# Opening layer 1's output projection with causal heads' tiles, and transposing the memory's probabilities into the scores' banks

## The chip, the core and the metric

One core of a Trainium2 chip runs the kernel as one launch. The metric is device microseconds (us) of that core. The engines named below are TensorE (PE: matmuls and transposes; PEld is its weight load), VectorE (DVE), ScalarE (ACT), GpSimd (POOL) and SyncE (SP, which here only issues transfers). PE writes its results into PSUM, eight banks of 128 partitions x 512 floats; ACT and DVE read them from there into SBUF.

## What is computed

The reference is a trunk of two layers over 256 positions of width 1024. Each layer has a mixer and, beside it, a 4-head cross-attention into 256 memory tokens; their outputs stand side by side, an output projection multiplies them, and a LayerNorm and a SwiGLU channel mixer follow. Layer 1's mixer is causal attention with 12 heads of 64 (256 positions are a single block, so it is plain causal attention):

```
q, k, v, q_mem = jnp.split(x @ b_w_in, [768, 1536, 2304], axis=-1)
mix     = causal_attention(q, k, v)                  # 12 heads x 64 -> 768 columns
mem_out = memory_cross_attention(q_mem, mem, w_kv)   # 4 heads x 64 -> 256 columns
sub = jnp.concatenate([mix, mem_out], axis=-1) @ w_mix_out
x = layer_norm(ALPHA * x + sub)
x = layer_norm(ALPHA * x + swiglu(x, w_ffn_in, w_ffn_out))
```

## The kernel before

Everything is float32, done on PE in reduced-precision passes: an operand is split into a high part (ACT, line 221) and a low part (DVE, line 222, which needs the high part), and a product takes three matmuls, high x high, high x low, low x high (`PASSES`). So each weight half of 128 x 1024 costs ACT and DVE one instruction each, and so does each activation tile. PE's order is the order of the code; the other engines' orders are set by a scheduler when the kernel is built, and each engine takes its instructions strictly in its order.

PSUM is two groups of four banks. `mm_tile` gives a bank of the group `mm` (projections, transposes, attention outputs), `acc_tile` one of the group `acc` (scores, the K projections, the output projection's sums). A new tile takes a bank whose tile before has been read by its last reader, and waits for that reader.

Layer 1's attention runs over six pairs of heads, i = 0 to 5 ("block i" below), in this order on PE: `qk_half(i, 0)`, the pair's Q (tile `qk`, 24 matmuls); `att_t(i-2)`, six transposes of the pair's probabilities (`pt`, line 849), which ACT copies to SBUF (`pT`, 851); `scores(i-1)`, two tiles `s` of five matmuls each, of which the second multiplies by `klq`, the low part of K that DVE makes (447); `qk_half(i, 1)`, the pair's K; `att_pv(i-2)`, the output `pv` of a pair, split into the pair's tile `mix` by ACT and DVE. The softmax of a score tile is maxima `mb` on DVE (370), exponentials `pb` on ACT (372) and a normalisation on DVE (377).

The memory's four heads are woven in: scores `sm` in blocks 1 and 3, eight transposes `ptm` (line 397, two tiles) in blocks 2 and 4, each copied by ACT to `pTm` (400), and in block 5 `mem_pv`, 16 matmuls `pvm`, whose two tiles become mix 6 and mix 7.

Then comes the output projection `OutProj(1, mix, "c")`, tile `opc`. For each half of the positions (`tt`) it adds up eight products, k = 0 to 7: k = 0 to 5 read the causal pairs' mix tiles, 6 and 7 the memory's. `op.step(tt, ks)` issues six matmuls for each k of the list; `op.close` issues the last two k and the LayerNorm. Pairs 4 and 5 are not done when it begins, so their transposes, scores and outputs are woven between its steps. The channel mixer (`pg`, `Xg`, `Yg`, `Zg`, `fog`) follows, then the last LayerNorm.

Of the kernel before, what the change touches and what calls it, by code (L numbers as in the profile page):

```python
# [208 lines left out]
def build(nc, tc, ins, out):  # L209
    ET = mybir.EngineType  # L210
    with (
# [15 lines left out]
        def mm_tile(name):  # L227
            return ps.tile([P, 512], F32, tag="mm", name=name)

        def work_tile(name):  # L230
            return actp.tile([P, 512], F32, tag="work", name=name, bufs=9)
# [122 lines left out]
        def load_gb(l, which):  # L354
            t = actp.tile([P, 2, D], F32, tag="gb", name=f"gb{l}{which}")
            nc.sync.dma_start(t[:, 0, :], bcast_row(ins[f"ln_{which}_g"][l, :], D))
            nc.sync.dma_start(t[:, 1, :], bcast_row(ins[f"ln_{which}_b"][l, :], D))
            return t
# [21 lines left out]
        def mem_scores(qa, k, nm, psum_tile, hs=range(4)):  # L380
            ka, kl = k
            pr = []
            for h in hs:
                c, par = h // 2, h % 2
                s = psum_tile[h - hs[0]](f"s{nm}{h}")
                for q in range(2):
                    score_mms(s[:, q * 256:(q + 1) * 256], qa[c][:, par, q * P:(q + 1) * P], ka[c][:, par, :], kl[:, c, par, :])
                pr.append(Softmax(s, [(0, 256), (256, 512)], f"{nm}{h}"))
            return pr

        def mem_transposes(pr, nm, hs=range(4)):
            pts = []
            for h in hs:
                t = mm_tile(f"ptm{nm}{h}")
                for q in range(2):
                    for k in range(2):
                        nc.tensor.transpose(t[:, k * 256 + q * P:k * 256 + (q + 1) * P],
                                            pr[h].p[:, q * 256 + k * P:q * 256 + (k + 1) * P], ident)
                sb = work_tile(f"pTm{nm}{h}")
                nc.scalar.copy(sb, t)  # L400
                pts.append(sb)
            return pts

        def mem_pv(pts, vm, mix, nm):
            for pair in range(2):
                o = mm_tile(f"pvm{nm}{pair}")
                for k in range(2):
                    for j in range(2):
                        h = 2 * pair + j
                        mm(o[HD * j:HD * j + HD, :T], vm[:, k, h * HD:(h + 1) * HD], pts[h][:, k * 256:(k + 1) * 256],  # L410
                           k == 0, k == 1)
                split(mix[6 + pair][:, 0, :], mix[6 + pair][:, 1, :], o[:, :T])
# [318 lines left out]
        for j in range(4):  # L731
            t = actp.tile([P, 2, 512], F32R, tag="hm", name=f"memT{j}", bufs=4)
# [28 lines left out]
        pr = mem_scores(qm, km, "m0", (acc_tile, acc_tile, mm_tile, mm_tile))  # L761
# [4 lines left out]
        op = OutProj(0, mix, "a")  # L766
# [5 lines left out]
        gb = load_gb(0, "mix")  # L772
        op.step(0, [2, 3, 4, 5])
        pts = mem_transposes(pr, "0")
        op.step(1, [0], first=True)
        mem_pv(pts, vm, mix, "0")
# [40 lines left out]
        def qk_half(hp, j):  # L817
            t = (acc_tile if j else mm_tile)(f"qk{hp}{j}")[:, :T].rearrange("p (j t) -> p j t", j=1)
            ws_proj(t, f"qk{hp}", xs, (j,))
            t = t[:, 0, :]  # L820
            if j == 0:
                st = actp.tile([P, 2, 512], F32R, tag="hm", name=f"qks{hp}", bufs=4).rearrange("p a (b t) -> p a b t", b=2)
                qks[hp] = st, klq[:, hp % 2]
                stack_q(lambda par: st[:, 0, par, :], t)
            else:
                stream.done(f"qk{hp}")
                st, kl = qks[hp]
                stack_k(lambda par: st[:, 1, par, :], kl, t)

        def scores(hp):  # L830
            st, kl = qks[hp]
            ss = []
            for par in range(2):
                s = acc_tile(f"s{hp}{par}")
                q, k = st[:, 0, par, :], st[:, 1, par, :]
                mm(s[:, 0:128], q[:, 0:128], k[:, 0:128], True, False)
                mm(s[:, 0:128], q[:, 0:128], kl[:, par, 0:128], False, False)
                mm(s[:, 128:384], q[:, 128:256], k, False, False)
                mm(s[:, 128:384], q[:, 128:256], kl[:, par], False, False)
                mm(s.rearrange("p (b t) -> p b t", t=256)[:, :, 0:128], identb, maskb.to_broadcast([P, 2, P]), False, True)  # L840
                ss.append(s)
            return [Softmax(s, [(0, 128), (128, 384)], f"b{hp}{j}") for j, s in enumerate(ss)]

        def att_t(hp):
            pts = []
            for j in range(2):
                t = mm_tile(f"pt{hp}{j}")
                for c in range(3):
                    nc.tensor.transpose(t[:, c * P:(c + 1) * P], prs[hp][j].p[:, c * P:(c + 1) * P], ident)
                sb = work_tile(f"pT{hp}{j}")  # L850
                nc.scalar.copy(sb[:, :384], t[:, :384])
                pts.append(sb)
            return pts

        def att_pv(hp):
            o = mm_tile(f"pv{hp}")
            for j in range(2):
                h = 2 * hp + j
                rows = slice(j * HD, (j + 1) * HD)
                mm(o[rows, 0:256], vt[:, 0, h * HD:(h + 1) * HD], pTs[hp][j][:, 0:256], True, False)  # L860
                mm(o[rows, 128:256], vt[:, 1, h * HD:(h + 1) * HD], pTs[hp][j][:, 256:384], False, True)
            split(mix[hp][:, 0, :], mix[hp][:, 1, :], o[:, :256])

        pts, pr_mem = [], []
        for i in range(6):
            qk_half(i, 0)
            if i >= 2:
                pTs[i - 2] = att_t(i - 2)
            if i >= 1:
                prs[i - 1] = scores(i - 1)  # L870
                for p in prs[i - 1]:
                    p.normalise()
            qk_half(i, 1)
            if i >= 2:
                att_pv(i - 2)
            if i in (1, 3):
                pr_mem += mem_scores(qm, km1, "m1", (acc_tile, acc_tile), (i - 1, i))
                for p in pr_mem[i - 1:]:
                    p.normalise()
            if i in (2, 4):  # L880
                pts += mem_transposes(pr_mem, "1", (i - 2, i - 1))
            if i == 2:
                gb = load_gb(1, "mix")
            if i == 4:
                mix += [actp.tile([P, 2, T], F32R, tag=f"mix{k}", name=f"mix1_{k}") for k in range(6, KT)]
            if i == 5:
                mem_pv(pts, vm1, mix, "1")
        op = OutProj(1, mix, "c")
        op.step(0, [6, 7], first=True)
        pTs[4] = att_t(4)  # L890
        prs[5] = scores(5)
        for p in prs[5]:
            p.normalise()
        op.step(0, [0])
        att_pv(4)
        op.step(0, [1])
        pTs[5] = att_t(5)
        op.step(0, [2])
        att_pv(5)
        op.step(1, [6], first=True)  # L900
        op.step(0, [3])
        op.close(0, [4, 5], xres, gb)
        op.step(1, [7, 0, 1, 2, 3])
        x3T = actp.tile([P, KT, 2, T], F32R, tag="xT", name="x3T")
# [81 lines left out]
```

## Time and profile before

| | us |
|---|---|
| median of 3 runs | 573.89 (573.73 to 576.27) |
| the profiled execution, its own time | 573.57 |
| span of its trace | 571.8 |
| PE busy | 558.6 (98% of the span) |
| DVE busy | 486.5 (85%) |
| ACT busy | 349.5 (61%) |

The span is the time from the first to the last instruction of the trace; the execution's own time holds 1.77 us more around it. Positions in the trace are counted from the span's start. PE's busy share counts a matmul as busy to its modelled end; matmuls overlap, so the next one starts a little before the one ahead of it ends.

### The profile page before, as it was taken

Reading aid. Unit: us, or ns where it says so; the run is one execution under the profiler, and the core shown is the slowest. Engines: PE = TensorE matmul, PEld = TensorE weight load, DVE = VectorE, ACT = ScalarE, POOL = GpSimd, SP = SyncE. Lnnn points to the kernel's source line nnn. Section 1 sums busy time; section 2 is a strip of 40 time slices with the busy share of each in tenths; the row PEclk is TensorE's granted clock in tenths of the full one; section 3 lists DMA queues with packets and bytes.
Section 4 is the critical chain, followed back from the end, with each engine's and each line's share of the span. In section 5 each row is a group of like instructions: output and inputs, shape, how many; then the busy total and the mean of one; then the engine's idle time right before and its main releaser. Section 6 shows DMA issues by size and latency. Waiting matters only on the chain.

```text
span 571.8 us, 8069 instructions
## 1 busy us (share of the span) xinstructions
PE 558.6 (98%) x3088; PEld 483.1 (84%) x3088; DVE 486.5 (85%) x649; ACT 349.5 (61%) x536; POOL 14.8 (3%) x24
## 2 busy tenths in 40 slices
PE   8999999999999999999999998899999999999994
PEld 7999879888888888888999997688888888888884
DVE  5797989999898998974987887489999999989726
ACT  6766957758647655852476988455656676558400
POOL 2020000000000000000100000000000000000001
PEclk9999999999999999999999999999999999999998
DMA  8997686416914932864476323247009629528002
GB/s 299 388 339 292 230 331 238 175 56 237 384 41 151 364 148 76 295 217 148 159 285 246 120 88 134 74 143 286 15 17 394 250 74 359 230 83 285 0 1 73
DMA packets 20182, 110.49 MB, mean 193 GB/s; under 512 B 2224, under 2 KB 5424, under 8 KB 8752
## 3 DMA queue, kind: packets, MB, share of 16 engines
q1 hardware_dynamic: 19856, 109.72, 52.0%
q8 instruction: 24, 0.39, 0.3%
q10 hardware_dynamic: 288, 0.26, 0.1%
q14 instruction: 14, 0.11, 0.1%
HBM read 108.92 MB, written 1.05 MB: 192 GB/s over the span
## 4 chain that ended last, share of the span: by engine, by line
PE 89%; ACT 4%; DVE 4%; issue 1%; DMA 1%; SPq 0%; POOLq 0%; ACTq 0%
PE fof L245 10%; PE pf L245 10%; PE pg L245 10%; PE fog L245 9%; PE Xf L245 6%; PE Xg L245 6%; PE opc L245 4%; PE opa L245 4%; PE pu L245 3%; PE bv L245 3%; PE Zg L245 3%; PE Zf L245 3%; PE va L245 3%; PE pvm L245 2%; PE hkm L245 2%; PE hqm L245 2%
## 5 line engine op out<-in xcount | busy, mean ns | idle before, releaser
L221 ACT CAST spl_s_M<-raw_s 128x1024 fp32r<-128x1024 f32 x84 | 86.7, 1054 | 52.9 <-DVE raw_s L179 23.3
L222 DVE TENSOR_TENSOR spl_s_M<-raw_s,spl_s_M 128x1024 fp32r<-128x1024 f32 x84 | 100.4, 1222 | 7.5 <-ACT spl_s_M L221 7.3
L245 PE MATMUL fof<-spl_w,htf 128*128 128x512 f32 x264 | 62.8, 390 | 0.0
L222 DVE TENSOR_TENSOR spl_w<-raw_w,spl_w 128x1024 fp32r<-128x1024 f32 x44 | 53.7, 1224 | 6.8 <-ACT spl_w L221 5.6
L245 PEld LDWEIGHTS fof<-spl_w,htf 128*128 128x128 f32 x264 | 49.4, 188 | 10.2
L179 DVE TENSOR_TENSOR raw_s<-raw_s,raw_s 128x1024 f32<-128x1024 f32 x48 | 57.0, 1220 | 0.0
L221 ACT CAST spl_w<-raw_w 128x1024 fp32r<-128x1024 f32 x44 | 46.1, 1053 | 15.9 <-PE fof L245 5.0
L245 PE MATMUL fog<-spl_w,htg 128*128 128x512 f32 x228 | 54.2, 390 | 0.0
L245 PEld LDWEIGHTS fog<-spl_w,htg 128*128 128x128 f32 x228 | 42.7, 188 | 8.8
L245 PE MATMUL qk<-x2T,spl_qk 128*128 128x256 f32 x288 | 36.7, 285 | 0.0
L245 PEld LDWEIGHTS qk<-x2T,spl_qk 128*128 128x128 f32 x288 | 35.2, 192 | 0.0
L245 PE MATMUL pf<-spl_r_A,x1T 128*128 128x512 f32 x120 | 29.2, 394 | 0.0
L245 PE MATMUL pg<-spl_r_A,x3T 128*128 128x512 f32 x120 | 29.1, 392 | 0.0
L245 PE MATMUL pg<-spl_r_B,x3T 128*128 128x512 f32 x120 | 28.9, 391 | 0.0
L221 ACT CAST spl_r_B<-raw_r_B 128x1024 fp32r<-128x1024 f32 x20 | 21.1, 1053 | 12.4 <-PE opc L245 6.2
L245 PE MATMUL pf<-spl_r_B,x1T 128*128 128x512 f32 x120 | 28.3, 389 | 0.0
L245 PEld LDWEIGHTS pf<-spl_r_B,x1T 128*128 128x128 f32 x120 | 22.5, 188 | 4.7
L222 DVE TENSOR_TENSOR spl_r_B<-raw_r_B,spl_r_B 128x1024 fp32r<-128x1024 f32 x20 | 24.4, 1219 | 2.4 <-ACT spl_r_B L221 2.3
L245 PEld LDWEIGHTS pg<-spl_r_B,x3T 128*128 128x128 f32 x120 | 22.4, 188 | 4.6
L245 PEld LDWEIGHTS pg<-spl_r_A,x3T 128*128 128x128 f32 x120 | 22.3, 188 | 4.5
L245 PEld LDWEIGHTS pf<-spl_r_A,x1T 128*128 128x128 f32 x120 | 22.2, 188 | 4.6 <-PE pvm L245 0.2
L245 PE MATMUL opc<-spl_o,mix 128*128 128x512 f32 x96 | 23.7, 399 | 1.7 <-ACT mix L221 1.7
(235 smaller groups left out, 1097.0 us busy)
## 6 DMA issues: line engine op xcount, KB each, us to landing
raw_s<-in_w SPq DMA_DIRECT2D x24, 1024.0 KB, 5.4
raw_w<-in_w SPq DMA_DIRECT2D x22, 1024.0 KB, 5.3
raw_r_A<-in_w SPq DMA_DIRECT2D x10, 1024.0 KB, 5.6
raw_r_B<-in_w SPq DMA_DIRECT2D x10, 1024.0 KB, 4.8
raw_o<-in_w SPq DMA_DIRECT2D x8, 1024.0 KB, 6.2
raw_qk<-in_w SPq DMA_DIRECT2D x6, 1024.0 KB, 4.8
raw_u<-in_w SPq DMA_DIRECT2D x3, 1024.0 KB, 9.7
raw_bv<-in_w SPq DMA_DIRECT2D x4, 768.0 KB, 4.3
```

Source lines behind the costliest of these rows:

```text
L179: self.nc.vector.tensor_add(raw, raw, self.raw[parts[1]][:, sl])
L221: nc.scalar.copy(hi, src)
L222: nc.vector.tensor_sub(lo, src, hi.bitcast(F32))
L245: nc.tensor.matmul(o, lhsT, rhs, start=start, stop=stop, skip_group_check=on)
```

## The change

It does two things. In blocks 2 and 4 the memory's transposes `ptm` take their PSUM tiles from the group `acc` in place of `mm` (layer 0's stay in `mm`). And the steps of the output projection's first half stand in another order: k = 0 and 1 open it where 6 and 7 did, then 2, 3, 6 and 7 stand at the four later places where 0, 1, 2 and 3 stood. The second half's order (6, then 7, 0, 1, 2, 3) and both closings stay.

```diff
-        def mem_transposes(pr, nm, hs=range(4)):
+        def mem_transposes(pr, nm, hs=range(4), psum_tile=mm_tile):
             pts = []
             for h in hs:
-                t = mm_tile(f"ptm{nm}{h}")
+                t = psum_tile(f"ptm{nm}{h}")
...
             if i in (2, 4):
-                pts += mem_transposes(pr_mem, "1", (i - 2, i - 1))
+                pts += mem_transposes(pr_mem, "1", (i - 2, i - 1), acc_tile)
...
         op = OutProj(1, mix, "c")
-        op.step(0, [6, 7], first=True)
+        op.step(0, [0, 1], first=True)
         pTs[4] = att_t(4)
         prs[5] = scores(5)
         for p in prs[5]:
             p.normalise()
-        op.step(0, [0])
+        op.step(0, [2])
         att_pv(4)
-        op.step(0, [1])
+        op.step(0, [3])
         pTs[5] = att_t(5)
-        op.step(0, [2])
+        op.step(0, [6])
         att_pv(5)
         op.step(1, [6], first=True)
-        op.step(0, [3])
+        op.step(0, [7])
         op.close(0, [4, 5], xres, gb)
```

The number of instructions is the same on every engine, and the orders of ACT, DVE, POOL and SP are the same. On PE the steps move, and the semaphores for which its instructions wait change.

First place, on PE: the end of block 4 and the start of block 5, from the second memory tile's first transpose to block 5's K projection, with the semaphores that a row waits for in brackets (most rows without a wait are left out; `ident` is the unit matrix, `pm` and `pb` are the memory's and the pairs' probabilities). Before:

```order
L397 MATMUL ptm_3395<-ident,pm_3256 128x128 [waits DVE_49,PE_49]
L245 MATMUL qk_3404<-x2T,spl_qk_0_3405 128x256 [waits DVE_49]
L849 MATMUL pt_3442<-ident,pb_3330 128x128 [waits DVE_49]
L849 MATMUL pt_3448<-ident,pb_3337 128x128 [waits Activation_49]
L245 MATMUL s_3454<-qks_3301 128x128
L245 MATMUL s_3460<-qks_3301 128x128
L245 MATMUL s_3460<-klq,qks_3301 128x128 [waits DVE_49]
L245 MATMUL qk_3486<-x2T,spl_qk_0_3405 128x256 x12
```

With the change:

```order
L397 MATMUL ptm_3395<-ident,pm_3256 128x128 [waits DVE_49,PE_49,Activation_49]
L245 MATMUL qk_3404<-x2T,spl_qk_0_3405 128x256 x12
L849 MATMUL pt_3442<-ident,pb_3330 128x128 [waits DVE_49] x2
L849 MATMUL pt_3448<-ident,pb_3337 128x128 [waits DVE_49] x2
L245 MATMUL s_3454<-qks_3301 128x128 [waits PE_49,Activation_49]
L245 MATMUL s_3454<-klq,qks_3301 128x128 [waits DVE_49]
L245 MATMUL s_3460<-qks_3301 128x128 [waits Activation_49]
L245 MATMUL s_3460<-klq,qks_3301 128x128 [waits DVE_49]
L245 MATMUL qk_3486<-x2T,spl_qk_0_3405 128x256 [waits Activation_49]
```

Before, the first `pt` waits until DVE has split `pv` of pair 2 and the second until ACT has copied the first `ptm` tile; with the change both wait for their own probabilities alone. In their place the second `ptm` tile waits until ACT has read the score tile of pair 3 (its exponentials), the second score tile until ACT has copied the first `ptm` tile, and the K projection until it has copied the second. Block 2 changes in the same way at its `ptm`.

Second place, on PE: the end of `mem_pv` and the start of the output projection, again without most of the rows that wait for nothing. Before:

```order
L245 MATMUL pvm_3531<-pTm_3400,svm_1143 64x256
L245 MATMUL opc_3538<-spl_o_3_0_3566,mix_6_3402 128x512 [waits Activation_49]
L245 MATMUL opc_3538<-spl_o_3_0_3566,mix_6_3402 128x512 [waits DVE_49]
L245 MATMUL opc_3538<-spl_o_3_1_3575,mix_7_3403 128x512 [waits Activation_49]
L245 MATMUL opc_3538<-spl_o_3_1_3575,mix_7_3403 128x512 [waits DVE_49]
L849 MATMUL pt_3586<-ident,pb_3466 128x128 x3
L849 MATMUL pt_3592<-ident,pb_3473 128x128 [waits PE_49]
```

With the change:

```order
L245 MATMUL pvm_3531<-pTm_3400,svm_1143 64x256
L245 MATMUL opc_3538<-spl_o_0_0_3542,mix_0_2779 128x512
L245 MATMUL opc_3539<-spl_o_0_0_3542,mix_0_2779 128x512 [waits PE_49,Activation_49]
L245 MATMUL opc_3538<-spl_o_0_1_3551,mix_1_2780 128x512
L849 MATMUL pt_3562<-ident,pb_3466 128x128 [waits DVE_49] x2
L849 MATMUL pt_3568<-ident,pb_3473 128x128 [waits DVE_49]
L245 MATMUL s_3574<-qks_3437 128x128 [waits Activation_49]
```

The four waits for the high and low parts of mix 6 and 7 are gone from the opening. The second matmul's wait is for pair 4's exponentials, the second `pt` tile's for DVE's low part of mix 3.

## Rows read from the trace of the kernel before

**Rows 1.** The page: busy time by engine, and the last chain's shares.

```profile
PE 558.6 (98%) x3088; PEld 483.1 (84%) x3088; DVE 486.5 (85%) x649; ACT 349.5 (61%) x536; POOL 14.8 (3%) x24
...
PE 89%; ACT 4%; DVE 4%; issue 1%; DMA 1%; SPq 0%; POOLq 0%; ACTq 0%
```

**Rows 2.** Chain that ended last: start, us, what; two of the pieces before 359.

```profile
315.96 0.97 PE sm L245 x8
...
358.61 0.38 ACT mix L221
```

**Rows 3.** Windows: length, busy us of each engine, granted clock, DMA share, GB/s.

```profile
345.00:359.00 14.00, 10.80 (x91) 9.16 (x89) 11.33 (x27) 12.61 (x35) 0.00 (x0) 1.00 0.22 81
```

**Rows 4.** Timeline of PE: start, duration, line, operation, idle time before and releaser.

```profile
344.17 1.09 PE L397 MATMUL ptm<-ident,pm 128*128 128x128 f32 x8
...
348.72 0.55 PE L849 MATMUL pt<-ident,pb 128*128 128x128 f32 x3 [0.59 <-DVE mix L222]
350.16 0.55 PE L849 MATMUL pt<-ident,pb 128*128 128x128 f32 x3 [0.90 <-ACT pTm L400]
...
351.19 0.28 PE L245 MATMUL s<-klq,qks 128*128 128x128 f32 x1
...
351.64 3.11 PE L245 MATMUL qk<-x2T,spl_qk 128*128 128x256 f32 x24
...
355.38 1.90 PE L245 MATMUL pvm<-pTm,svm 128*64 128x256 f32 x16
359.03 3.22 PE L245 MATMUL opc<-spl_o,mix 128*128 128x512 f32 x12 [1.74 <-ACT mix L221]
362.08 0.82 PE L849 MATMUL pt<-ident,pb 128*128 128x128 f32 x6
...
366.19 1.69 PE L245 MATMUL opc<-spl_o,mix 128*128 128x512 f32 x6
367.71 0.82 PE L849 MATMUL pt<-ident,pb 128*128 128x128 f32 x6
```

**Rows 5.** Timeline of ACT, block 4 to the projection's start.

```profile
344.46 0.46 ACT L372 ACTIVATE pb<-s,mb 128x256 f32<-128x256 f32 x1
...
349.52 1.07 ACT L400 COPY pTm<-ptm 128x512 f32<-128x512 f32 x2
...
358.61 0.65 ACT L221 CAST mix<-pvm 128x256 fp32r<-128x256 f32 x2
```

**Rows 6.** Timeline of DVE in the same stretch.

```profile
350.01 0.43 DVE L447 TENSOR_TENSOR klq<-qk,qks 64x256 fp32r<-64x256 f32 x1
...
359.30 0.42 DVE L222 TENSOR_TENSOR mix<-pv,mix 128x256 fp32r<-128x256 f32 x1
359.64 0.75 DVE L222 TENSOR_TENSOR mix<-pvm,mix 128x256 fp32r<-128x256 f32 x2
```

**Rows 7.** The chain in the channel mixer: one piece of 24 matmuls.

```profile
410.01 5.44 PE fog L245 x24
```

**Rows 8.** Timelines in block 2: ACT's exponential and copies, PE's transposes.

```profile
325.44 0.46 ACT L372 ACTIVATE pb<-s,mb 128x256 f32<-128x256 f32 x1
...
330.82 0.84 ACT L851 COPY pT<-pt 128x384 f32<-128x384 f32 x2
...
329.04 0.82 PE L849 MATMUL pt<-ident,pb 128*128 128x128 f32 x6
```

**Rows 9.** Timelines after the projection's start: who feeds PE, and how early.

```profile
372.35 1.05 ACT L221 CAST spl_r_B<-raw_r_B 128x1024 fp32r<-128x1024 f32 x1 [1.21 <-PE opc L245]
...
409.41 0.69 DVE L222 TENSOR_TENSOR htg<-tpg,htg 128x512 fp32r<-128x512 f32 x1
...
410.75 0.62 PE L245 MATMUL fog<-spl_w,htg 128*128 128x512 f32 x2
...
428.81 1.22 DVE L222 TENSOR_TENSOR spl_s_M<-raw_s,spl_s_M 128x1024 fp32r<-128x1024 f32 x1
...
433.44 0.39 PE L245 MATMUL Xg<-spl_s_M,SgM 128*128 128x512 f32 x1
```

## The prediction, as it stood before the run

> **What bounds the kernel now.** I read the page first: PE is busy for 98% of the span and holds 89% of the chain that ended last, ACT and DVE 4% each [rows 1]. So a microsecond counts only where PE waits, and the next question is where the chain leaves PE. It does so in layer 1's attention: after the memory's scores, a piece that ends at 316.93, no PE piece stands on the chain until ACT's split of mix 6 ends at 358.99 and the projection starts [rows 2]. In between PE runs ahead of ACT and DVE, and pays at the end. In the window 345 to 359 PE is busy 10.80 of 14 us, ACT 12.61, and TensorE's granted clock stays at 1.00, its level of 2.4 GHz, so the idle time has no second price in clock [rows 3]. PE's timeline names the three waits: 0.59 us before `pt` for DVE's split of mix 2, 0.90 before the second `pt` for ACT's copy `pTm`, 1.74 before the first `opc` for ACT's mix 6 [rows 4]. They add up to 3.23 us; after the projection's start I found no further one, and the chain is PE again.
>
> **The opening of the projection.** It waited for mix 6 and needs mix 0 and 1 now, whose pairs were split in blocks 2 and 3; the weight halves it reads were made before too, and no DMA moves, since SP's order is the same. `pvm` starts at 355.38 and its modelled end is 357.28; `opc`'s row shows how much earlier than that a successor starts: it ends at 362.25, while `pt` stands at 362.08, 0.17 before. So `opc` could have started at 357.11 and started at 359.03: 1.92 us go [rows 4]. The twelve matmuls then took 3.05 us start to start, with a second small wait inside for mix 6's low part (DVE's row of both low parts begins at 359.64) [rows 6]. Six unhindered ones take 1.52 (366.19 to 367.71), and six more at the channel mixer's pace, 24 in 5.44 us, take 1.36 [rows 4, 7]. That is 2.88 in place of 3.05: another 0.17. Bounds: 0 and 0.33, twelve at 2.72. The new second matmul's wait, for pair 4's exponentials, costs nothing, since ACT has gone on from them to the splits of mix 6 and 7 by 358.61 [rows 5] and had them done before it took up the weight casts between.
>
> **The waits in blocks 4 and 5.** The two waits before `pt` go; others stand in their place. ACT and DVE keep their orders, and nothing in this stretch lets them start earlier: their chain is their own [rows 2]. So I hold their times and move PE alone. ACT copies the two `ptm` tiles from 349.52 to 350.59 [rows 5], the first one ending just before the `pt` at 350.16 that waited for it [rows 4]. With the change PE does both `pt` and the first score tile before that, but the second score tile now wants that very bank: it too starts at about 350.16. Its second matmul wants `klq`, done at 350.44 [rows 6]; with the 0.05 us from release to start it goes at 350.49 in place of 351.19 [rows 4]. The K projection behind it comes out at 350.94, later than the second copy's end, so that its own new wait is covered by 0.35 us. Worth: **0.70**, not the 1.49 of the two waits. Bounds: 0 (the K projection or the score tile held until its old time) and 1.49.
>
> **What the new banks cost.** In block 4 the second `ptm` tile waits for ACT's exponentials of pair 3, which end at 344.92; the eight transposes begin at 344.17, so the fifth came at about 344.66, and some 0.3 us are lost [rows 4, 5]. They fall in front of the wait until 350.16 and are absorbed by it. In block 2 the same exponential ends at 325.90, and again about 0.3 us are lost on PE. PE is not on the chain there: the next thing ACT takes from it, the `pt` tiles that end at 329.86, lies ready for 0.96 us before ACT copies them at 330.82 [rows 8]. So I cost both at nothing; with that cover gone they would be 0.6.
>
> **What is late next.** With `opc` 0.70 + 1.92 us earlier, at 356.41, and 2.88 long, the transposes of pair 4 start at 359.29. The second of their tiles waits for DVE's low part of mix 3, done at 359.72 [rows 6]; PE gets there at about 359.6, so with a restart this costs 0.20, and what stands behind it, pair 5's scores and the rest of the steps, is late by as much. Bound: 0 to 0.4. After that the old distances hold: mix 6 and 7, whose low parts end at 360.39 [rows 6], are read some 4 us later, and the pieces between two steps have the same lengths as before.
>
> **Does the rest follow?** ACT waits for PE at 372.35, for a weight buffer to come free [rows 9], so the feeding of the channel mixer starts earlier with PE. If it did not: the tightest weight half I found is done at 430.03 and used at 433.44, 3.4 us of room [rows 9], more than is gained. The tightest loop through DVE is shorter: `htg`'s low part ends at 410.10 and is used at 410.75, 0.65 us [rows 9]; it begins with PE, so it should move as a whole.
>
> **The sum.** 0.70 + 1.92 + 0.17 - 0.20 = 2.59 us. From the execution's own 573.57 (span 571.8 and 1.77 around it) that leaves 570.98; from the median, 0.32 higher, 571.30. I predict **571.2**. With the terms at their bounds it is 0 + 1.74 + 0 - 0.4 = 1.34 (572.2) to 1.49 + 1.92 + 0.33 = 3.74 (569.8).
>
> **Rivals.** *All waits go* (569.8): the copies of `ptm` no longer hold anything, because the tiles have banks of their own. The Trainium skill, page "Perfetto Trace Analysis", section "Optimizing Tensor Performance", says so: independent matmul groups should rotate through PSUM banks so that the evacuation of one overlaps the next group's matmuls; by that the block-4 term would be 1.49 where the rows give 0.70. Against it: the bank that the second score tile and the K projection take is the one that ACT empties at 350.10 and 350.59, and ACT is busy 12.61 of those 14 us [rows 3, 5]. The rotation only moves the wait to another tile.
>
> *Given back later* (572.9): if DVE's work in the channel mixer did not move with PE, the loop with 0.65 us of room would take back 1.94. DVE's 85% [rows 1] speaks for it, ACT's wait for PE at 372.35 against.
>
> *No effect* (573.6): some wait that I don't see takes the opening's place. The new one on pair 4's exponentials would be it, and ACT's order speaks against.
>
> *Slower*: the second `ptm` copy becomes what PE waits for. Before, that copy held nothing until `pvm`; now the K projection of pair 5 stands behind it, and behind that `pv`, `pvm` and the whole projection. Each microsecond that ACT comes to it later than 350.94 goes onto the end. It decides from 0.35 + 2.59 = 2.94 us of delay on; 6 us would give 576.6. For it speaks that ACT is the busiest engine there but PE; against it that no instruction of ACT or DVE before the copy waits for anything that the change delays by more than 0.3 us, with 0.96 us of room in block 2 [rows 8].
>
> **Numbers.** My forecast 0.66 (own range 570.5 to 571.9), all waits go 0.10, given back 0.14, no effect 0.06, slower 0.04. The range takes the forecast, the first rival and most of the second: 569.8 to 572.9. A measurement of this kernel tells about 0.5%, 2.87 us, from no change; the forecast stands just inside it at 2.59. I give it one chance in five to be over that, 0.13, and with the first rival faster comes to 0.23; slower 0.03, three quarters of that rival; the rest, 0.74, is the same.
>
> **What would show it.** Right: no idle time before the first `opc`; the wait of 0.9 before the second `pt` gone and a new one of some 0.4 to 0.8 before the second score tile, released by ACT's `pTm`, with `klq` behind it; the first `opc` near 356.4, the first step between 366 and 372 some 2.6 us earlier; ACT's copies still at 349.5 and mix 6 at 358.6. The forecast falls if those ACT times move (then its chain did depend on PE), if PE shows idle time after 372, or if the K projection starts at 351.6 as before.

## The result, and the profile after

The changed kernel takes **571.12 us** (median of 8, 570.58 to 571.95) where the kernel before takes 573.83 (median of 8), ratio 0.9947 with an interval of 0.9934 to 0.9960. Two more series of it gave 571.31 and 571.00 (ratios 0.9948 and 0.9940). 571.2 was forecast. All three intervals lie below 1, so the changed kernel is faster, by about half a per cent; the prediction took 0.5% for the least that can be told from no change, and the gain stands right at that.

Executions of one and the same kernel differ by some 3 us, in those with a profile mostly because the first weights land at another time in each (the last section shows the largest case). This lies ahead of everything that the change touches. In the profiles it can be taken off: the first `sm` matmul of layer 1's memory scores stands ahead of the change's first instruction, and the distance from it to the span's end holds no start. In 11 of the 14 profiles this matmul stands 306.96 to 307.00 us behind the first one on the low part of the second weight piece, wherever that one is. Kernel before and kernel after, PE's timeline at that matmul (start, duration, what):

```profile
315.79 0.28 PE L245 MATMUL sm<-kkm,qqm 128*128 128x256 f32 x1
```

```profile
315.41 0.28 PE L245 MATMUL sm<-kkm,qqm 128*128 128x256 f32 x1
```

With the spans of 571.8 and 568.8 the distances are 256.01 and 253.39 us: **2.62 us** by the change, and 0.38 of the 3.0 between the two spans by the start. Two more profiles of the changed kernel, with the first `sm` at 316.17 and 315.86, give 253.43 and 253.44. The distance repeats within 0.05 us, which is also how far a span, given to 0.1 us, can be off. So below it is the measure for what the clock times can't tell apart.

The page of after: busy time, and the shares of the chain that ended last [answers to rows 1].

```profile
PE 559.4 (98%) x3088; PEld 484.2 (85%) x3088; DVE 486.4 (86%) x649; ACT 349.7 (61%) x536; POOL 15.3 (3%) x24
...
PE 93%; DVE 3%; ACT 2%; DMA 1%; issue 1%; SPq 0%; POOLq 0%; ACTq 0%
```

Window of 14 us at the same place, 0.38 earlier [rows 3]: length, busy us of PE, PEld, DVE, ACT, POOL, then granted clock, DMA share, GB/s.

```profile
344.62:358.62 14.00, 13.66 (x105) 11.77 (x104) 11.36 (x27) 12.61 (x34) 0.00 (x0) 1.00 0.22 85
```

PE is busy 13.66 of the 14 us, not 10.80; ACT's busy time is the same 12.61. PE's timeline of after [rows 4]:

```profile
344.16 1.13 PE L397 MATMUL ptm<-ident,pm 128*128 128x128 f32 x8
345.05 3.11 PE L245 MATMUL qk<-x2T,spl_qk 128*128 128x256 f32 x24
348.00 0.82 PE L849 MATMUL pt<-ident,pb 128*128 128x128 f32 x6
348.57 0.30 PE L245 MATMUL s<-qks 128*128 128x128 f32 x1
...
349.73 0.33 PE L245 MATMUL s<-qks 128*128 128x128 f32 x1 [0.33 <-ACT pTm L400]
350.07 0.33 PE L245 MATMUL s<-klq,qks 128*128 128x128 f32 x1
...
350.56 3.11 PE L245 MATMUL qk<-x2T,spl_qk 128*128 128x256 f32 x24
353.60 0.88 PE L245 MATMUL pv<-pT,vt 128*64 128x256 f32 x8
354.30 1.90 PE L245 MATMUL pvm<-pTm,svm 128*64 128x256 f32 x16
356.14 3.02 PE L245 MATMUL opc<-spl_o,mix 128*128 128x512 f32 x12
358.99 0.91 PE L849 MATMUL pt<-ident,pb 128*128 128x128 f32 x6
359.66 0.30 PE L245 MATMUL s<-qks 128*128 128x128 f32 x1
...
360.25 0.31 PE L245 MATMUL s<-qks 128*128 128x128 f32 x1
360.39 0.28 PE L245 MATMUL s<-klq,qks 128*128 128x128 f32 x1
...
360.83 1.63 PE L245 MATMUL opc<-spl_o,mix 128*128 128x512 f32 x6
```

Of the three waits none is left; one of 0.33 stands before the second score tile, released by ACT's copy `pTm` (the prediction named 0.4 to 0.8 as its sign). The first `opc` waits for nothing. ACT's timeline [rows 5]:

```profile
349.09 1.07 ACT L400 COPY pTm<-ptm 128x512 f32<-128x512 f32 x2
...
358.19 0.65 ACT L221 CAST mix<-pvm 128x256 fp32r<-128x256 f32 x2
```

Both are 0.42 or 0.43 earlier than before, which is the start's 0.38 and 0.05: ACT kept its own pace while PE moved by 2.6.

### The profile page after: what moved, and what is told of

It is laid out like the page before. It is cut to its first block, busy times and chain, and to the rows that moved or that the text cites. A ratio compares the mean times of both kernels' runs of the same rounds, so it can differ in the third digit from the quotient of the medians.

```text
span 568.8 us, 8070 instructions
## 1 busy us (share of the span) xinstructions
PE 559.4 (98%) x3088; PEld 484.2 (85%) x3088; DVE 486.4 (86%) x649; ACT 349.7 (61%) x536; POOL 15.3 (3%) x24
## 4 chain that ended last, share of the span: by engine, by line
PE 93%; DVE 3%; ACT 2%; DMA 1%; issue 1%; SPq 0%; POOLq 0%; ACTq 0%
PE fof L245 11%; PE pf L245 10%; PE pg L245 10%; PE fog L245 9%; PE Xg L245 6%; PE Xf L245 6%; PE opc L245 4%; PE opa L245 4%; PE qk L245 4%; PE pu L245 3%; PE bv L245 3%; PE Zf L245 3%; PE Zg L245 3%; PE pvm L245 3%; PE va L245 3%; PE hkm L245 2%
## 5 line engine op out<-in xcount | busy, mean ns | idle before, releaser
L221 ACT CAST spl_r_A<-raw_r_A 128x1024 fp32r<-128x1024 f32 x20 | 20.7, 1050 | 6.2 <-PE opa L245 4.3
```

Of the source, the lines that this page charges most:

```text
L221: nc.scalar.copy(hi, src)
```

## The experiments

"First sm" is its start in the run's profile, "distance" the span less that start, "gain" 256.01 less the distance. The first four ran beside 17 runs of the kernel before (median 573.77), the next four beside 17 (574.12), the last four beside 16 (574.64). These three medians differ although the kernel is one, so the ratios of different groups are not compared.

| kernel | median us | ratio, interval | first sm | distance | gain |
|---|---|---|---|---|---|
| banks only | 575.04 | 1.0011, 0.9999 to 1.0023 | 315.77 | 255.93 | 0.08 |
| order only | 571.75 | 0.9960, 0.9945 to 0.9975 | 316.11 | 253.99 | 2.02 |
| the change again | 571.31 | 0.9948, 0.9935 to 0.9962 | 316.17 | 253.43 | 2.58 |
| K first | 571.00 | 0.9945, 0.9932 to 0.9959 | 316.68 | 253.22 | 2.79 |
| four more in block 2 | 571.80 | 0.9963, 0.9950 to 0.9976 | 316.48 | 254.02 | 1.99 |
| copies twice | 572.42 | 0.9979, 0.9964 to 0.9995 | 318.81 | 254.39 | 1.62 |
| opening of three | 572.29 | 0.9979, 0.9965 to 0.9994 | 316.16 | 254.14 | 1.87 |
| one tile in acc | 571.14 | 0.9951, 0.9936 to 0.9966 | 315.56 | 253.44 | 2.57 |
| K between | 571.74 | 0.9957, 0.9942 to 0.9972 | 315.91 | 254.09 | 1.92 |
| four more in block 4 | 570.99 | 0.9939, 0.9925 to 0.9953 | 315.87 | 253.43 | 2.58 |
| eight more in block 4 | 571.16 | 0.9945, 0.9931 to 0.9960 | 315.99 | 253.41 | 2.60 |
| the change, third time | 571.00 | 0.9940, 0.9928 to 0.9953 | 315.86 | 253.44 | 2.57 |

### Half of the change: the banks alone

```diff
-        op.step(0, [0, 1], first=True)
+        op.step(0, [6, 7], first=True)
...
-        op.step(0, [2])
+        op.step(0, [0])
...
-        op.step(0, [3])
+        op.step(0, [1])
...
-        op.step(0, [6])
+        op.step(0, [2])
...
-        op.step(0, [7])
+        op.step(0, [3])
```

> The banks of the change with the old order of the steps (the projection opens with mix 6 and 7). Theory (the terms of the prediction): the two waits before pt go and the second score tile's wait takes their place, so TensorE is about 0.7 us further at pvm; but the first opc still waits for ACT's mix 6, which ACT makes at 358.6 whatever TensorE does, so the wait before opc grows from 1.74 to about 2.4 us and the time stays at 573.8 (gain 0, at most 0.2). Rival (the parts add up, each wait removed is worth its length): 0.7 us less, 573.1.

PE's timeline of it, the last product of the attention and the projection's start:

```profile
354.64 1.90 PE L245 MATMUL pvm<-pTm,svm 128*64 128x256 f32 x16
358.94 3.19 PE L245 MATMUL opc<-spl_o,mix 128*128 128x512 f32 x12 [2.40 <-ACT mix L221]
```

`pvm` stands 0.72 earlier than before (38.87 behind the first `sm`, before 39.59), and the wait for mix 6 has grown by 0.66 to 2.40. What was won in block 5 is waited away at the projection: a gain of 0.08, hardly more than the reading's error. The theory holds. The clock times say it too, once they are looked at one by one: 5 of the 12 lie at 573.3 to 573.6 and 7 at 575.0 to 576.1, where of the 17 of the kernel before 14 lie at 573.4 to 574.1 and 3 at 575.0 to 575.4; so its median fell among the upper ones. The profiled execution, 573.44, is of the lower.

### The other half: the order alone

```diff
-                pts += mem_transposes(pr_mem, "1", (i - 2, i - 1), acc_tile)
+                pts += mem_transposes(pr_mem, "1", (i - 2, i - 1))
```

> The new order of the steps with the old banks. Theory: the waits of 0.59 and 0.90 us before pt stay, the 1.74 before opc goes, opc starts at about 357.1 by the positions of the kernel before, its twelve matmuls take 2.88, and the pt behind them come at 360.0, after DVE's low part of mix 3, so that no wait stands there: 1.92 + 0.17 = 2.09 us less, 571.7. Rival 1 (the parts add, so what the whole change gave over the banks' 0.7 is the order's): 573.8 - 1.9 = 571.9, with a wait before pt. Rival 2 (the banks give nothing): as the whole change, 571.1.

PE's timeline of it:

```profile
349.04 0.55 PE L849 MATMUL pt<-ident,pb 128*128 128x128 f32 x3 [0.59 <-DVE mix L222]
350.47 0.55 PE L849 MATMUL pt<-ident,pb 128*128 128x128 f32 x3 [0.89 <-ACT pTm L400]
...
355.69 1.90 PE L245 MATMUL pvm<-pTm,svm 128*64 128x256 f32 x16
357.53 3.02 PE L245 MATMUL opc<-spl_o,mix 128*128 128x512 f32 x12
360.38 0.81 PE L849 MATMUL pt<-ident,pb 128*128 128x128 f32 x6
362.13 1.63 PE L245 MATMUL opc<-spl_o,mix 128*128 128x512 f32 x6
```

The two waits of block 5 stand as before, the opening has none, and neither have the `pt` behind it (1.75 to the next `opc`, as before). 2.02 us of gain, 2.09 expected. So the parts don't add: 0.08 and 2.02 alone, 2.6 together. The banks are worth 0.6 only when the projection no longer waits for the memory.

### The changed kernel again

> The changed kernel itself once more, timed beside the others. Theory: of the 3.0 us between the two profiled executions 0.4 came from the landing of the second raw_v piece at the start (it differs from run to run), 2.6 from the change: 571.2, ratio 0.9955; in its profile the last opc piece before the channel mixer lies 2.6 us earlier than before, once the difference at the start is taken off. Rival: the change gives 3.0 by itself: 570.8, ratio 0.9947, and 3.0 in the profile after the start is taken off.

> The changed kernel once more, beside the version with K between the score tiles: 571.2, and counted from the first sm the last piece of opc 2.6 us earlier than in the kernel before, whatever the first sm's own place is. Rival (the place of the first sm and the gain hang together): another distance than in the two profiles of it that there are.

2.58 and 2.57 at two other starts, 571.31 and 571.00 in clock time: the change gives 2.6, and the rest of the 3.0 between the first two profiles came from the start.

### The copies' hold taken away, or doubled

```diff
-                t = psum_tile(f"ptm{nm}{h}")
+                t = (mm_tile if (nm, h) == ("1", 2) else psum_tile)(f"ptm{nm}{h}")
```

> The change, but block 4's first ptm tile takes its bank from mm again and only the second from acc: then the second score tile no longer waits for ACT's first copy. Theory (the prediction's: klq stands right behind): the second pt tile waits for DVE's low part of mix 2 some 0.2 to 0.4 us, the score tile's second matmul still starts with klq, and from there all is as in the change: gain 0 to 0.1. Rival (all waits go, once no copy holds a bank): the 0.33 and what stands behind it go, 0.3 to 0.5 us less than the change, 570.8.

PE's timeline of it, block 5:

```profile
348.11 0.89 PE L849 MATMUL pt<-ident,pb 128*128 128x128 f32 x6
...
350.23 0.33 PE L245 MATMUL s<-klq,qks 128*128 128x128 f32 x1 [0.58 <-DVE klq L447]
...
350.72 3.11 PE L245 MATMUL qk<-x2T,spl_qk 128*128 128x256 f32 x24
```

The six `pt` hardly wait (0.89 for 0.82, where 0.2 to 0.4 were expected). The second score tile's first matmul is free, its second waits for `klq` at 34.67 behind the first `sm`, where it stood at 34.66 with the change, and the K projection starts at 35.16 after 35.15. Nothing is won: behind the copy stands `klq`, which DVE makes from what ACT has split.

```diff
-                nc.scalar.copy(sb, t)
+                for _ in range(2 if nm == "1" and h in (2, 3) else 1):
+                    nc.scalar.copy(sb, t)
```

> The change, with ACT's two copies of block 4's ptm tiles made twice, one behind the other: the order on ACT is first, second, first, second, so each bank comes free some 1.0 us later. Theory (this stretch still goes at ACT's pace after the change): the second score tile starts 1.0 us later, its wait grows from 0.33 to about 1.3, and all behind it is 0.95 to 1.05 us later: 572.2. Rival (the copies hold nothing until 2.94 us of delay, as the prediction's slower rival has it for the K projection): 571.2, as the change.

ACT's copies, then PE's timeline of it, block 5 and behind the projection's opening:

```profile
352.52 2.05 ACT L401 COPY pTm<-ptm 128x512 f32<-128x512 f32 x4
```

```profile
353.58 0.30 PE L245 MATMUL s<-qks 128*128 128x128 f32 x1 [0.76 <-DVE klq L448]
...
354.16 3.11 PE L245 MATMUL qk<-x2T,spl_qk 128*128 128x256 f32 x24
...
363.75 0.55 PE L850 MATMUL pt<-ident,pb 128*128 128x128 f32 x3 [0.67 <-DVE mix L222]
```

The distance is 0.95 longer than the 253.44 of the change: a microsecond of ACT goes to the end. That is the size that the theory has, but it came by another way, so the number does not bear the theory out. The second score tile does not start 1.0 later, only 0.45 (34.77 behind the first `sm`, with the change 34.32), and its first matmul waits for `klq`, not for a copy. Its bank is then not the one that the first copy holds: with two reads more the banks came out otherwise, and this run does not test the copy's hold on the score tile. The K projection is late by only 0.20 (35.35 behind the first `sm`). The other 0.75 comes at the second `pt` of pair 4, which waits for DVE's low part of mix 3; DVE starts on that 0.99 later than with the change (44.46 behind the first `sm`, 43.47).

The prediction's slower rival let 0.35 us of ACT's delay go free and put every further microsecond onto the end; its 2.94 us is where the whole gain would be used up, and not, as the rival of this run reads it, where a loss begins. The copies end 1.01 us later here (35.76 behind the first `sm`, 34.75 with the change), which by that account costs 0.66. It cost 0.95, and most of it not at the K projection: the wait that the prediction priced at 0.20 is the next door that closes.

### More matmuls ahead of the wait

```diff
-                for q in range(2):
+                for q in [0, 1] * (2 if nm == "1" and h == 0 else 1):
```

> The change, with the four transposes of block 2's first ptm tile issued twice: four more, 0.54 us more of TensorE. Theory (what is lost in block 2 is absorbed by the wait that is left in block 5): counted from the first sm, the second score tile starts where it does in the change, its wait of 0.33 is gone and the 0.2 for klq behind it nearly so; the end is 0.0 to 0.1 us later: 571.2 to 571.3. Rival (TensorE is busy 98% and every matmul more is paid): 0.54 later, 571.8, and the wait of 0.33 stays.

By the numbers the rival has it, 0.6 later and the wait of 0.33 still there. But the kernel differs in one thing more: its scheduler set DVE's instructions of block 3 in another order. DVE's timeline of the change, then of this kernel:

```profile
331.40 0.42 DVE L438 SCALAR_TENSOR_TENSOR qks<-qk,qks 64x256 fp32r<-64x256 f32 x1
331.85 0.62 DVE L370 TENSOR_REDUCE mb<-s 128x1 f32<-128x128 f32 x2
332.50 0.43 DVE L438 SCALAR_TENSOR_TENSOR qks<-qk,qks 64x256 fp32r<-64x256 f32 x1
332.94 0.62 DVE L370 TENSOR_REDUCE mb<-s 128x1 f32<-128x128 f32 x2
```

```profile
332.49 0.42 DVE L438 SCALAR_TENSOR_TENSOR qks<-qk,qks 64x256 fp32r<-64x256 f32 x1
333.36 0.43 DVE L438 SCALAR_TENSOR_TENSOR qks<-qk,qks 64x256 fp32r<-64x256 f32 x1 [0.45 <-ACT qks L437]
333.80 1.15 DVE L370 TENSOR_REDUCE mb<-s 128x1 f32<-128x128 f32 x4
```

The first maxima stood between the two low parts of Q and now stand behind both, where DVE waits 0.45 for ACT. PE's own Q projection behind the eight and more transposes is 0.07 later; the first maximum is 0.88 later, and from there everything is 0.62 later, the last wait included. So the run doesn't decide the question it was made for. It points to another thing: two instructions of DVE changed about, beside matmuls of which PE's own timeline shows only 0.07, go with a loss nearly as large as the whole term of blocks 4 and 5. No run changes DVE's order alone, so that it is the cause is read from the trace and not shown. The same test in block 4, where the orders of ACT and DVE stay as they are, was run with the second tile twice (h == 3), and with both:

```diff
-                for q in range(2):
+                for q in [0, 1] * (2 if nm == "1" and h in (2, 3) else 1):
```

> The change, with the four transposes of block 4's second ptm tile issued twice: 0.54 us more of TensorE, and the orders of ACT and DVE as they are (the same test in block 2 changed DVE's order). Theory: the room of 0.51 us (0.33 before the second score tile, 0.18 before its second matmul) takes it in; from block 5's K projection on all lies 0.0 to 0.1 us later than in the change, counted from the first sm. Rival (TensorE is the bound and every matmul is paid): 0.54 later, and the 0.33 stays.

> The same with both ptm tiles of block 4: eight transposes more, 1.09 us of TensorE. Theory: 0.51 is taken in as with four, and what is over is paid at once: 0.5 to 0.6 later from the K projection on, no wait left before the score tile, and the wait of 0.1 before the second pt behind the projection's opening goes too, so 0.45 to 0.55 at the end. Rival (all is paid): 1.09.

PE's timeline with eight more, the Q and the K projection of block 5:

```profile
346.45 3.12 PE L245 MATMUL qk<-x2T,spl_qk 128*128 128x256 f32 x24
...
351.15 3.12 PE L245 MATMUL qk<-x2T,spl_qk 128*128 128x256 f32 x24
```

Eight transposes make the Q projection 0.82 late (30.46 behind the first `sm`, 29.64 in the change), and the K projection starts at 35.16, 0.01 later. Four make it 0.44 late, and the K projection stands at 35.16 as well. Both distances to the end are those of the change. Absorption is shown, in block 4. With eight, neither the 0.5 us of the theory nor the 1.09 of the rival came: the room was larger than I had read from the timeline. Its "idle before" counts from the modelled end of the last matmul. Start to start the loss is larger: in the change the second score tile begins 1.16 behind the first, where pair 5's begins 0.59 behind (359.66 to 360.25), and its second matmul 0.34 behind where 0.14 is enough: 0.57 + 0.20 = 0.77, not 0.33 + 0.18.

### Versions that might have been better

```diff
+            if i == 5:
+                qk_half(i, 1)
             if i >= 1:
                 prs[i - 1] = scores(i - 1)
...
-            qk_half(i, 1)
+            if i < 5:
+                qk_half(i, 1)
```

> The change, and in block 5 the K projection stands ahead of pair 4's scores. Theory: what is left of TensorE's waiting there is 0.33 us for ACT's copy of ptm and about 0.2 for klq; with 3 us of K projection in front both lie behind it, and 0.5 us more go: 570.6. Rival: pair 4's scores come 3 us later, DVE's normalisation of them ended at 355.3 and now ends at about 358.5 or later, among the weight splits and the mix tiles, and the pt that need it (at 358.5 then) wait for it: 0.5 to 1.5 us are lost behind opc, 571.1 to 572.1.

PE's timeline of it, the projection's opening:

```profile
356.59 0.50 PE L245 MATMUL opc<-spl_o,mix 128*128 128x512 f32 x1
357.52 2.81 PE L245 MATMUL opc<-spl_o,mix 128*128 128x512 f32 x11 [0.43 <-ACT pb L372]
```

`pvm` starts 38.07 behind the first `sm` where the change has 38.89, so what block 5 still lost (0.77, above) is won, and then the second `opc` waits for the bank that ACT's late exponentials of pair 4 hold: the first step takes 3.58 to the next `pt`, not 2.85. 0.2 is left by the distance, less than the clock times can show (571.00 and 571.31 side by side). The scheduler set other orders on ACT and DVE here too (ACT casts two weight halves ahead of pair 4's exponentials), so not all of this need be the K projection's new place.

The second version puts the K projection between the two score tiles.

```diff
+                if between and par == 0:
+                    between()
...
-                prs[i - 1] = scores(i - 1)
+                prs[i - 1] = scores(i - 1, (lambda: qk_half(5, 1)) if i == 5 else None)
```

> The change, with block 5's K projection between the two score tiles of pair 4. Theory: the first score tile and ACT's exponentials of it stay early, so that the second opc does not wait for its bank as it did where the whole K projection stood first; the second score tile comes 3 us later and waits for nothing. About 0.5 us of TensorE's waiting goes at the score tile and 0.1 to 0.3 may come back before the second pt of pair 4: 0.2 to 0.5 less than the change, 570.9. Rival (what was won is waited for again behind, as there): 0 to 0.15 less, 571.2.

PE's timeline of it, the second `pt` tile of pair 4:

```profile
360.44 0.61 PE L851 MATMUL pt<-ident,pb 128*128 128x128 f32 x3 [0.67 <-DVE pb L377]
```

It lost 0.65 against the change. `pvm` came 0.21 earlier (38.68 behind the first `sm`), but then the second head's probabilities are normalised too late, and the second `pt` waits 0.67 for them. The second score tile waits for nothing, as expected; the wait of 0.33 for ACT's copy has passed to the K projection, which takes the bank now.

The third opens the projection with three products (k = 0, 1, 2, then 3, 6, 7 at the next three places).

```diff
-        op.step(0, [0, 1], first=True)
+        op.step(0, [0, 1, 2], first=True)
...
-        op.step(0, [2])
+        op.step(0, [3])
...
-        op.step(0, [3])
+        op.step(0, [6])
...
-        op.step(0, [6])
+        op.step(0, [7])
...
-        op.step(0, [7])
```

> The change, with the opening of the projection three products long (k = 0, 1, 2) and 3, 6, 7 behind it. Theory: the 1.5 us more ahead of pair 4's transposes cover the wait of their second tile for mix 3's low part, the pt come back to 0.57 us to the first score matmul, and nothing else waits: 0.1 us less than the change, 571.1. Rival: the 0.1 are no wait for mix 3 but TensorE's own, and stay: 571.2; or the closing comes to mix 5 too early, since one step less stands ahead of it, and waits some tenths: 571.5.

PE's timeline of it, behind the opening and in the channel mixer's first block:

```profile
361.11 0.81 PE L849 MATMUL pt<-ident,pb 128*128 128x128 f32 x6
362.86 1.63 PE L245 MATMUL opc<-spl_o,mix 128*128 128x512 f32 x6
...
392.95 1.29 PE L346 MATMUL ptc<-ident,xres 128*128 128x128 f32 x8 [0.31 <-DVE xres L338]
```

The wait at the `pt` is gone as expected (1.75 to the next `opc`, with the change 1.84), so it was a wait for mix 3 and not PE's own time. But 0.7 are lost 30 us later, in the second half's LayerNorm, where the transposes `ptc` wait for DVE: with the other place of the steps the scheduler put weight splits between DVE's instructions of that LayerNorm. None of the three beats the changed kernel measurably.

## Why the prediction was right

**By terms**, each as a distance between two starts on PE, before and after:

| term | forecast | before | after | measured |
|---|---|---|---|---|
| blocks 4 and 5: first `sm` to the K projection | 0.70 | 35.85 | 35.15 | 0.70 |
| opening: `pvm` to the first `opc` | 1.92 | 3.65 | 1.84 | 1.81 |
| the twelve `opc` | 0.17 | 3.05 | 2.85 | 0.20 |
| `pt` of pair 4 to the next `opc` | -0.20 | 1.75 | 1.84 | -0.09 |
| sum | 2.59 | | | 2.62 |

The sum is nearer than its terms: 0.11 too much at the opening and 0.11 too much for mix 3's wait cancel, and that is luck.

The step that carried most was to hold ACT's and DVE's times and to move PE alone; ACT's copies and its mix 6 stayed, against the first `sm`, within 0.05 us. So the second score tile could be placed at 350.16, its second matmul at 350.49 and the K projection at 350.94; after adding the 0.38 of the start they stand at 350.11, 350.45 and 350.94. The opening was 0.11 too large: 16 `pvm` need 1.84 to the next start, not 1.73. I had taken from an `opc` row that a successor starts 0.17 before the modelled end; behind the 1.90 of `pvm` it starts 0.06 before it. Mix 3's wait cost 0.09 and not 0.20; "opening of three", where it is gone, showed that it was this wait. Mix 6 and 7 are read 5.30 us behind their low parts (359.97 to 365.27), not some 4; nothing hung on that.

**What the new banks cost.** In block 2 PE lost 0.37 against the first `sm` (its Q projection starts at 326.07 with the change and at 326.08 before, although the start was 0.38 earlier), where 0.3 were forecast, and in block 4 only 0.05 more, since it came there 0.37 later. Both vanish in block 5's wait. The absorption was shown for block 4 by experiment. In block 2 the experiment was spoilt by DVE's order; what speaks for it there is that the block 5 term came out whole at 0.70, and that ACT's copies and mix 6 stand no later than before although PE was 0.37 late.

**Given back later** is refuted: from the piece of `opc` behind pair 5's output to the span's end it is 201.16 us before (370.64 to 571.8) and 201.17 after (367.63 to 568.8). The loop with 0.65 us of room moved as a whole: DVE's low part of `htg` starts at 406.40, 2.63 earlier once the start's 0.38 is taken off:

```profile
406.40 0.68 DVE L222 TENSOR_TENSOR htg<-tpg,htg 128x512 fp32r<-128x512 f32 x1
```

**No effect** falls with it; the wait for pair 4's exponentials that it named is real, and cost 0.7 where "K first" made them late.

**All waits go** is refuted too, at the place where it was forecast to differ: 0.70 and not 1.49. The Trainium skill, page "Perfetto Trace Analysis", section "Optimizing Tensor Performance", has matmul groups rotate through banks so that emptying one overlaps the next group. Here the rotation won less than half of the 1.49: the wait passed to the second score tile, whose bank ACT's copy holds. With that bank free ("one tile in acc") the K projection starts no earlier (35.16 behind the first `sm`, 35.15 with the change), since ACT and DVE make the operands besides emptying the banks, and `klq` is done no sooner. The **slower** rival did not come, as ACT's times did not move; its account of where a delay of ACT would be paid was wrong, as told at the doubled copies: at the wait for mix 3 more than at the K projection.

What stays open: the 0.08 of "banks only", and how much more block 2 could absorb. Mix 6 came 0.07 earlier in "banks only"; behind the first `sm` it stands at 42.82 before and 42.81 with "order only", at 42.75 to 42.78 with the new banks, so this goes with the banks, and I don't know how.

## What to carry to other kernels

When one engine runs ahead of a pair of others that keep their own pace, hold the slow ones' times fixed, slide the fast one along them, and ask at each release what it finds next; that gave each term here within 0.11 us, though not the way that a delay of ACT would take. A saving ahead of a later wait is worth next to nothing until that wait goes as well: 0.08 and 2.02 alone were 2.6 together. And where a scheduler orders an engine, compare its order before believing an experiment: two changed-about DVE instructions came with a loss of 0.62 us, more than what was to be measured.

## What the hardware showed that was not expected

The times of one kernel lie in two groups some 1.7 us apart (most clearly those of "banks only", above). The profiled run of "copies twice" (574.97, with a median of 572.42) shows how one comes about. PE at its start, and windows behind it (columns as above):

```profile
9.25 0.62 PE L245 MATMUL va<-spl_v,x0T 128*128 128x384 f32 x2 [1.88 <-ACT spl_v L221]
10.24 2.01 PE L245 MATMUL va<-spl_v,x0T 128*128 128x384 f32 x8 [0.38 <-DVE spl_v L222]
```

```profile
10.00:12.00 2.00, 1.76 (x8) 1.76 (x9) 1.87 (x5) 1.79 (x4) 0.00 (x0) 0.84 1.02 380
12.00:14.00 2.00, 2.00 (x8) 2.00 (x8) 1.99 (x3) 1.62 (x4) 0.00 (x0) 0.50 1.05 392
14.00:16.00 2.00, 2.00 (x11) 2.00 (x10) 1.90 (x5) 1.81 (x4) 0.00 (x0) 0.81 1.01 397
16.00:18.00 2.00, 2.00 (x13) 2.00 (x12) 1.98 (x3) 1.04 (x2) 0.00 (x0) 1.00 1.02 426
```

The second weight piece landed late, PE waited 1.88 us for it and 0.38 once more, and from 12 to 14, with PE busy again, the granted clock stands at 0.50, its level of 1.2 GHz; by 16 it is back at 1.00. The first `sm` stands 3.40 us later than in the profile of after: 1.81 of it at the landing (10.24 against 8.43) and 1.59 behind, about the time that the clock withheld in the windows (0.32 + 1.00 + 0.38 = 1.70 us). In the 13 other profiles, with waits of at most 1.23 there, the clock from 10 to 30 us was 1.00. The other runs of the upper group have no trace, but their mean granted clock is on record. The 13 other profiled executions have 0.995 to 0.998, this one 0.992. Of the 136 executions with a clock on record 22 have 0.992 to 0.994, and each of these lies 1.57 us or more above the shortest of its series; five others lie as high with 0.995 or 0.996. So most of the upper group had a lower clock, as this one had, and for a few the cause stays open. Where in the run the clock fell, and what stood ahead of it, is seen in this one trace alone.
